# RWKV mixer on one core: inputs of gate and v formed ahead of the decay, joins of the inverse moved up among v's steps, bonus product placed behind the substitution

## The chip, the cores and the metric

The kernel runs as one program on one core of a Trainium2 chip. The metric is device time in microseconds (us), taken over three executions. Five engines run in parallel, each through its own instructions in order: TensorE (PE, matrix products and transposes, with its weight loads PEld), VectorE (DVE), ScalarE (ACT), GpSimd (POOL) and SyncE (SP), which issues the DMAs. They wait for each other by semaphores.

## The reference, cut to what matters

Two layers, each of two SwiGLU feed-forward blocks around a token mixer, and a gated embedding at the end. The second layer's mixer is RWKV-7, with x of 256 positions by 1,024 features, 16 heads of 64, in chunks of 64 positions. Only this mixer is touched:

```
dx = shift(h) - h
r, k, v = (h + dx*mu[n]) @ w_in[n]          # n = 0, 1, 2
xw, xa, xg = (h + dx*mu[n])                 # n = 3, 4, 5
decay = exp(-exp(-softplus(-(w0 + tanh(xw@w1)@w2)) - 0.5))
a = sigmoid(a0 + (xa@a1)@a2);  g = sigmoid(xg@g1) @ g2
kk = heads(k*k_k) / |heads(k*k_k)|;  k = k*(1 + (a-1)*k_a)
S_t = S_{t-1} diag(decay_t) + (S_{t-1} (-kk_t)) (kk_t a_t)^T + v_t k_t^T;  y_t = S_t r_t
bonus = sum(r*k*r_k) * v
out = ((groupnorm(y) + bonus) * g) @ w_out
```

## The kernel before, in words

Activations stand with features on the 128 partitions, eight blocks of 256 positions each. `xprod(n)` (L813) forms one of the six inputs `h + dx*mu[n]` in eight DVE instructions of 128x256, from hnT and dxT. The mixer forms k first (`K`, two halves b of 128 positions), and `knorm(b, ...)` (L889 to L904) normalises it: DVE multiplies out of PSUM, ACT squares, DVE sums and clamps (gn), POOL takes the power and scales. `ktr(b)` transposes the normalised and the plain k on PE. `low` and `l1` are the low-rank products of decay and a; `squares` and `decay` form the decay on ACT and DVE, with two scans (L987).

`r_step(k)` (L1051) is one eighth of r's product. Between its steps stands `triangle(i)`, the chunks' triangular matrices for half of the heads, copied out of PSUM by ACT (L1045, L1046). The inverse of each 64x64 unit triangle starts with a forward substitution on DVE over blocks of 16 (L1090 to L1093) and two transposes (L1094, L1095). Four `join(i)` then join blocks of 16 to 32 and to 64: tiny products on PE, issued in four pieces.

`v_step(k, between)` (L1300) is one eighth of v's product, four matrix products, each followed by one piece of `between`. `inside(k)` (L1274) forms the products within a chunk for one pair of heads (sc), masks them on DVE (L1287) and forms rb. `gate1`, `gate_t` and `gate2` form g; `gains` multiplies g with the norm's gains and the bonus sums of `bo_sums`, which reads k times r (L1269). `tb` transposes b and k and copies them into bn. `stack_v(c)` (L1386) subtracts the mean over 64 from chunk c's v and writes it into the stacked state sv; the means stand in vm (L1383, L1384). `chunk(c)` is the recurrence, four times: PE products, ACT and DVE copies into sv (L1443, L1444), and the state's update on DVE (L1458).

What orders the work: the kernel is written in one order, and a scheduler sets each engine's order from it, by dependences, priorities that follow the text, and estimated costs. `behind(name)` holds what it encloses back until the named instruction has been issued; L collects these names. Large tiles share 20 slots, handed out from a queue of free ones (`slot`, `drop`): a new tile waits until all users of the slot's former tile are done. PSUM's eight banks go round in the same way. `P` and `need` fetch weights: the DMA on SP, a copy on ACT (L154) and a subtraction on DVE (L156) that split each weight in two.

Of the kernel before, what the change touches and what calls it, by code (L numbers as in the profile page):

```python
# [15 lines left out]
D = 1024  # L16
T = 256
NB = 2
# [42 lines left out]
class Trunk:  # L61
# [730 lines left out]
    def rwkv(self, at):  # L792
# [20 lines left out]
        def xprod(n, lo=0, hi=T, ks=range(KT)):  # L813

            if n not in X["x"]:
                X["x"][n] = self.slot("xr")
            hv, dv = g8(X["hnT"]), g8(X["dxT"])
            for k in ks:
                V.scalar_tensor_tensor(xent(n, k)[:, lo:hi], dv[:, k, lo:hi], mu(n, k), hv[:, k, lo:hi], op0=ALU.mult, op1=ALU.add)
# [127 lines left out]
        lt = l1()  # L947
        self.drop(X["x"][3], X["x"][4])
        xprod(0)
        wu_ = self.slot("wu")  # L950
        zt = wu_[:, :1024]
        G.memset(zt, 0.0)
# [139 lines left out]
                            Wd[:, :, 0:t, 0:t].rearrange("p a s i -> p a i s"), op=ALU.mult)  # L1092
            V.tensor_reduce(Wd[:, :, t, 0:t], pr_, axis=AX.X, op=ALU.add)  # L1093
        V.transpose(wv.rearrange("p n s -> p s n"), Wu.rearrange("p t s -> p s t"))  # L1094
        V.transpose(xt.rearrange("p n t -> p t n"), Wu)  # L1095

        def pieces(n, do, last):

# [3 lines left out]
        def join(i):  # L1102

            if i == 0:
                ps = self.bank("q1")

                def do(ns):
                    for n in ns:
                        for o in range(0, 128, 32):
                            mm(ps[o:o + 32, n * 16:(n + 1) * 16], lhsT=nx[o:o + 16, n, :], rhs=wv[o:o + 16, n, 0:16], start=True, stop=True)  # L1110

                def last():
                    S.copy(qn[:, :, 0:16], ps.rearrange("p (n t) -> p n t", t=16))
                    self.unbank(ps)
            elif i == 1:
                ps = self.bank("x1")

                def do(ns):
                    for n in ns:
                        for o in range(0, 128, 32):  # L1120
                            mm(ps[o:o + 32, n * 16:(n + 1) * 16], lhsT=qn[o:o + 32, n, :], rhs=xt[o:o + 32, n, 16:32], start=True, stop=True)

                def last():
                    V.tensor_tensor(xt[:, :, 16:32], ps.rearrange("p (n t) -> p n t", t=16), xt[:, :, 16:32], op=ALU.add)
                    self.unbank(ps)
                    V.transpose(wu_[:, 1024:], md)
                    for o in range(0, 128, 32):
                        c0 = o // 32 % 2 * 32
                        (V.tensor_copy if c0 else S.copy)(xv[o:o + 32, :, c0:c0 + 32], xt[o:o + 32])
            elif i == 2:  # L1130
                ps = [self.bank("q2") for _ in range(2)]

                def do(ns):
                    for n in ns:
                        for o in (0, 64):
                            mm(ps[n // 16][o + 32:o + 64, n % 16 * 32:n % 16 * 32 + 32], lhsT=mo[o:o + 32, n * 32:(n + 1) * 32],
                               rhs=wv[o:o + 32, n, :], start=True, stop=True)

                def last():
                    for hh in range(2):  # L1140
                        for o in (0, 64):
                            (S.copy if o else V.tensor_copy)(qv[o + 32:o + 64, hh * 16:hh * 16 + 16, :], ps[hh][o + 32:o + 64].rearrange("p (n t) -> p n t", t=32))
                    self.unbank(*ps)
            else:
                ps = [self.bank("x2") for _ in range(2)]

                def do(ns):
                    for n in ns:
                        for o in (0, 64):
                            mm(ps[n // 16][o:o + 32, n % 16 * 32:n % 16 * 32 + 32], lhsT=qv[o + 32:o + 64, n, :], rhs=xt[o + 32:o + 64, n, :], start=True, stop=True)  # L1150

                def last():
                    for hh in range(2):
                        for o in (0, 64):
                            (S.copy if o else V.tensor_copy)(xv[o:o + 32, hh * 16:hh * 16 + 16, 32:64], ps[hh][o:o + 32].rearrange("p (n t) -> p n t", t=32))
                    self.unbank(*ps)
            return pieces(32, do, last)
# [90 lines left out]
        rT = self.slot("rT")  # L1248
        for g in range(4):
            S.copy(rT[:, g * 512:(g + 1) * 512], psr[g])  # L1250
        xprod(5)
        gate1()
        xprod(2)
        self.drop(hnT, dxT)
        for m in range(KT):
            S.activation(g8(av)[:, m], g8(av)[:, m], AF.Identity, scale=vec(3)[:, m:m + 1], bias=w0h[:, 8 + m:9 + m])
        V.tensor_tensor(kT, kT, av, op=ALU.mult)
# [7 lines left out]
        for g in range(4):  # L1265
            for h in range(2):
                S.copy(skv[g][half[h], :, h, :, 0:64], gs(ta, g)[half[h]])
                V.tensor_tensor(skv[g][half[h], :, h, :, 64:128], gs(rT, g)[half[h]], gs(gam, g)[half[h]], op=ALU.mult)
        V.tensor_tensor(kT, kT, rT, op=ALU.mult)  # L1269
        self.drop(gam, ta, rT)  # L1270
        rb_ = self.slot("rb")
        rbv = c4(rb_)

        def inside(k):  # L1274

            g, m = k // 2, k % 2
            if m == 0:
                X["rb"] = self.bank("rb")
            psb = X["rb"].rearrange("p (m c t) -> p m c t", m=2, c=4)
            ps = [self.bank("sc") for _ in range(2)]  # L1280
            pv = [t.rearrange("p (c t) -> p c t", c=4) for t in ps]
            for c in range(NCH):
                for h in range(2):
                    mm(pv[h][half[1 - h], c], lhsT=c4(kt)[half[h], k, c], rhs=skv[g][half[h], m, h, c, :], start=True, stop=True)  # L1284
            for h in range(2):
                ho = half[1 - h]
                V.tensor_tensor(skv[g][ho, m, h], pv[h][ho], mk[ho].unsqueeze(1).to_broadcast([64, 4, 128]), op=ALU.mult)  # L1287
            self.unbank(*ps)
            for c in range(NCH):
                for h in range(2):  # L1290
                    hh = half[h]
                    mm(psb[hh, m, c], lhsT=c4(bt)[hh, k, c], rhs=skv[g][hh, m, h, c, 64:128], start=True, stop=True)
            if m:
                V.tensor_tensor(c3(rb_[:, g * 512:(g + 1) * 512]), c3(X["rb"]), mk[:, 64:128].unsqueeze(1).to_broadcast([128, 8, 64]), op=ALU.mult)
                self.unbank(X["rb"])
# [4 lines left out]
        def v_step(k, between=()):  # L1300

            x = xent(2, k)
            w = self.need(at["v"] + k // 2)[0][:, k % 2]
            between = list(between)
            for b in range(NB):
                for q in range(2):
                    mm(psv[b][q], lhsT=x[:, b * 128:(b + 1) * 128], rhs=w[:, q * 512:(q + 1) * 512], start=k == 0, stop=k == KT - 1)  # L1307
                    if between:
                        between.pop(0)()
            if k % 2:  # L1310
                self.release(at["v"] + k // 2)
                if k < 5:
                    P(1, 1)
# [8 lines left out]
        v_step(2)  # L1322
        for n in gate2(1):
            n()
        v_step(3)
        v_step(4)
        xx = self.slot("xx")
        xv = xx.rearrange("p (n t) -> p n t", t=64)
        for o in (32, 96):
            G.memset(xv[o:o + 32, :, 0:32], 0.0)  # L1330
        v_step(5, join(0))
        inside(0)
        inside(1)
        v_step(6, join(1))
        self.drop(nq)
        bo_sums()
        gains()
        inside(2)
        inside(3)
        v_step(7, join(2))  # L1340
        self.drop(X["x"][2])
        vn = self.slot("vn")
        for b in range(NB):
            for q in range(2):
                S.copy(vn[:, b * D + q * 512:b * D + (q + 1) * 512], psv[b][q])
        self.unbank(*psv[0], *psv[1])
        inside(4)
        inside(5)

        bn = [self.slot("bn") for _ in range(2)]  # L1350
        bnv = [t.rearrange("p (c h m t) -> p c h m t", c=2, h=2, t=64) for t in bn]
# [21 lines left out]
        turn.pop(0)()  # L1373
        turn.pop(0)()
        self.drop(bt, kt)

        sv = [self.slot("sv") for _ in range(2)]
        svv = [t.rearrange("p (c m h t) -> p c m h t", c=2, m=8, h=2) for t in sv]
        vv = vn.rearrange("p (b m h t) -> p b m h t", b=2, m=8, h=2)
        vm = self.small(32, "vm", 1)  # L1380
        vmv = vm.rearrange("p (b m h) -> p b m h", b=2, h=2)
        for b in range(NB):
            V.tensor_reduce(vm[:, b * 16:(b + 1) * 16], vn[:, b * D:(b + 1) * D].rearrange("p (h t) -> p h t", t=64), axis=AX.X, op=ALU.add)  # L1383
            V.tensor_scalar(vm[:, b * 16:(b + 1) * 16], vm[:, b * 16:(b + 1) * 16], ck[:, 0:1], 1.0 / 64, op0=ALU.mult, op1=ALU.mult)  # L1384

        def stack_v(c):  # L1386
            rs = half[c % 2]
            for h in range(2):
                V.scalar_tensor_tensor(svv[c // 2][half[1 - h], c % 2, :, h, :], vv[rs, c // 2, :, h, :], ck[rs, 0:1],
                                       vmv[rs, c // 2, :, h].unsqueeze(2).to_broadcast([64, 8, 64]), op0=ALU.mult, op1=ALU.subtract)  # L1390

        for c in range(NCH):
            stack_v(c)
        G.memset(svv[0][EV, 0, :, 0, :], 0.0)
        G.memset(svv[0][OD, 0, :, 1, :], 0.0)

        yo = self.slot("yo")
        yv = yo.rearrange("p (b m h t) -> p b m h t", b=2, m=8, h=2)
# [136 lines left out]
            return ps  # L1535
        chunk(0)
        with behind("c"):
            P(1, 0)
            vgain(0)
        chunk(1)  # L1540
        with behind("c"):
            P(1, 0)
            vgain(1)
        self.drop(X["gn"], X["lg"])
# [135 lines left out]
```

## Time and profile before

| | |
|---|---|
| median of three executions | 1177.98 us (1177.35 to 1180.4) |
| profiled execution | 1183.38 us, span 1181.6 us |
| PE busy | 1151.2 us, 97% |
| DVE busy | 859.1 us, 73% |
| ACT busy | 659.7 us, 56% |
| POOL busy | 72.5 us, 6% |
| weight split on DVE (L156) | 348 times, mean 1223 ns |

Busy is the time in which an engine has an instruction running. The mixer lies in the span from about 745 to 960 us. Over the whole span PE is nearly always busy; in the mixer, stretches follow each other in which a different engine is full, so it has to be read by stretches. The granted clock (PEclk) is 1.00 at 2.4 GHz and 0.50 at 1.2 GHz.

### The profile page before, as it was taken

How to read it: one execution, taken by the hardware profiler on the slowest of the kernel's cores; microseconds unless marked ns; L12 is line 12 of the kernel's file. 1: busy time of each engine (PE TensorE's matmuls, PEld its weight loads, DVE VectorE, ACT ScalarE, POOL GpSimd, SP SyncE). 2: the span in 40 equal slices, each digit the busy share in tenths (PEclk: the TensorE clock that was granted, in tenths of full speed). 3: DMA queues.
4: the chain of work that ended last, by engine and by line, in shares of the span. 5: the costliest groups of instructions: out<-in, count | busy, mean ns of one | idle time of the engine just before them, and what ended most of it. 6: DMA issues, size and time to landing. Idle time of an engine off the chain costs nothing. (4 is left out here: it accounts for less than half of the span.)

```text
span 1181.6 us, 18709 instructions
## 1 busy us (share of the span) xinstructions
PE 1151.2 (97%) x7284; PEld 954.3 (81%) x7284; DVE 859.1 (73%) x1299; ACT 659.7 (56%) x1145; POOL 72.5 (6%) x92
## 2 busy tenths in 40 slices
PE   8999999999999999999999999999998899999997
PEld 6788888888888888888888888777467778888886
DVE  5886666877678666667876666878859898676663
ACT  6665556545476555558755554374226396555553
POOL 0000000010010000001100000230000220000011
PEclk8999999999999999999999999999989999999999
DMA  7886654746586666646766664550300377666510
GB/s 244 292 295 196 190 172 152 253 156 205 186 271 202 194 192 184 192 134 196 248 189 194 193 192 144 178 183 1 125 4 21 108 249 263 193 189 193 177 47 36
DMA packets 58841, 207.78 MB, mean 176 GB/s; under 512 B 6784, under 2 KB 7296, under 8 KB 58496
## 3 DMA queue, kind: packets, MB, share of 16 engines
q1 hardware_dynamic: 58752, 206.59, 54.8%
q8 instruction: 57, 0.93, 0.3%
q14 instruction: 32, 0.26, 0.1%
HBM read 205.51 MB, written 1.05 MB: 175 GB/s over the span
## 5 line engine op out<-in xcount | busy, mean ns | idle before, releaser
L156 DVE TENSOR_TENSOR w<-raw,w 128x1024 fp32r<-128x1024 f32 x348 | 423.6, 1223 | 145.6 <-ACT w L154 139.8
L154 ACT CAST w<-raw 128x1024 fp32r<-128x1024 f32 x348 | 366.3, 1055 | 153.9 <-PE mm L400 68.7
L400 PE MATMUL mm<-xT,w 128*128 128x512 f32 (+1 forms) x2304 | 407.8, 337 | 0.0
L400 PEld LDWEIGHTS mm<-xT,w 128*128 128x128 f32 x2304 | 358.6, 189 | 50.0
L178 PE MATMUL acc<-w,hT 128*128 128x512 f32 x352 | 138.2, 393 | 0.0
L179 PE MATMUL acc<-w,hT 128*128 128x512 f32 x352 | 137.3, 390 | 0.0
L180 PE MATMUL acc<-w,hT 128*128 128x512 f32 x352 | 137.1, 389 | 0.0
L408 ACT COPY pn<-mm 128x256 f32<-128x256 f32 x144 | 46.6, 375 | 93.8 <-PE mm L400 93.8
L409 DVE TENSOR_TENSOR pn<-mm,pn 128x256 f32<-128x256 f32 x144 | 54.4, 418 | 39.3 <-ACT pn L408 39.3
L180 PEld LDWEIGHTS acc<-w,hT 128*128 128x128 f32 x352 | 66.1, 188 | 14.1
L178 PEld LDWEIGHTS acc<-w,hT 128*128 128x128 f32 x352 | 66.2, 188 | 12.6
L179 PEld LDWEIGHTS acc<-w,hT 128*128 128x128 f32 x352 | 66.3, 188 | 12.3
L232 POOL TENSOR_SCALAR rpost<-ss 128x1 f32<-128x1 f32 x15 | 7.5, 500 | 777.9 <-ACT junk L239 777.9
L178 PE MATMUL mm<-w,xT 128*128 128x512 f32 x128 | 51.8, 415 | 2.9 <-ACT w L154 2.6
L289 DVE SCALAR_TENSOR_TENSOR xT<-tr,gT,xT 128x128 fp32r<-128x128 f32 x112 | 35.6, 344 | 24.4 <-ACT xT L288 23.5
L179 PE MATMUL mm<-w,xT 128*128 128x512 f32 x128 | 51.4, 405 | 0.7 <-DVE xT L289 0.5
L412 DVE TENSOR_TENSOR pn<-pn,yc 128x512 f32<-128x512 f32 x72 | 49.7, 691 | 2.0
L180 PE MATMUL mm<-w,xT 128*128 128x512 f32 x128 | 50.9, 403 | 0.0
L179 PE MATMUL z<-w,xT 128*128 128x512 f32 x128 | 49.9, 390 | 0.0
L180 PE MATMUL z<-w,xT 128*128 128x512 f32 x128 | 49.9, 390 | 0.0
L178 PE MATMUL z<-w,xT 128*128 128x512 f32 x128 | 49.7, 393 | 0.0
L288 ACT ACTIVATE xT<-tr,gT 128x128 fp32r<-128x128 f32 x112 | 37.8, 371 | 19.3 <-PE tr L275 14.9
(282 smaller groups left out, 1534.8 us busy)
## 6 DMA issues: line engine op xcount, KB each, us to landing
raw<-in_w SPq DMA_DIRECT2D x264, 512.0 KB, 4.3
raw<-in_win SPq DMA_DIRECT2D x32, 512.0 KB, 4.4
raw<-in_wout SPq DMA_DIRECT2D x16, 512.0 KB, 4.8
raw<-in_wg SPq DMA_DIRECT2D x16, 512.0 KB, 3.9
wf<-in_wrkv SPq DMA_DIRECT2D x8, 1024.0 KB, 5.1
gbc<-in_norm_g SPq DMA_DIRECT2D x9, 512.0 KB, 5.4
raw<-in_wrkv SPq DMA_DIRECT2D x8, 512.0 KB, 3.5
raw<-in_bwout SPq DMA_DIRECT2D x8, 512.0 KB, 3.6
```

Source lines behind the costliest of these rows:

```text
L154: self.high = self.nc.scalar.copy(hh, r[:p, :n])
L156: eng.tensor_tensor(ll, r[:p, :n], hh.bitcast(F32), op=ALU.subtract)
L178: mm(out, lhsT=lh, rhs=rh, start=start, stop=False)
L179: mm(out, lhsT=ll, rhs=rh, start=False, stop=False)
L180: mm(out, lhsT=lh, rhs=rl, start=False, stop=stop)
L232: nc.gpsimd.tensor_scalar(r, a, b, eps, op0=ALU.add, op1=ALU.add)
L288: done = (nc.scalar.activation(hi, v, AF.Copy, scale=gc), nc.vector.scalar_tensor_tensor(lo, v, gc, hi.bitcast(F32), op0=ALU.mult, op1=ALU ...
L289: nc.vector.scalar_tensor_tensor(lo, v, gc, hi.bitcast(F32), op0=ALU.mult, op1=ALU.subtract))
L400: nc.tensor.matmul(ps[i][:, :T] if s else ps[i], lhsT=w[:, sl], rhs=x, start=u + q + s == 0, stop=s + u == 2 and q == 3)
L408: nc.scalar.copy(zi, ps[i][:, T:])
L409: nc.vector.tensor_tensor(zi, ps[i][:, :T], zi, op=ALU.add)
L412: nc.vector.tensor_tensor(z2, z2, rbc.unsqueeze(1).to_broadcast([128, 2, T]), op=ALU.mult)
```

## The change

Five things are moved; no arithmetic is added or removed.

- `xprod(5)` and `xprod(2)`, the inputs of gate and v, stand behind `xprod(0)`, and hnT and dxT are dropped there.
- The joins 0, 1, 2 are carried by v's steps 3, 4, 5 instead of 5, 6, 7; `inside(4)` and `inside(5)` by steps 6 and 7.
- k times r stands behind the last transpose of the substitution (`behind("sub")`).
- The mean of the first half of v and the first two `stack_v` stand ahead of `tb`; the second mean and `stack_v(2)` behind chunk 0, `stack_v(3)` behind chunk 1.
- The slots are handed out in another order as a result, and with them the order of some weight loads.

```diff
@@ behind l1()
         xprod(0)
+        xprod(5)
+        xprod(2)
+        self.drop(hnT, dxT)
@@ the substitution
-        V.transpose(xt.rearrange("p n t -> p t n"), Wu)
+        L["sub"] = V.transpose(xt.rearrange("p n t -> p t n"), Wu)
@@ behind r
-        xprod(5)
         gate1()
-        xprod(2)
-        self.drop(hnT, dxT)
...
-        V.tensor_tensor(kT, kT, rT, op=ALU.mult)
-        self.drop(gam, ta, rT)
+        self.drop(gam, ta)
@@ v's steps
-        v_step(3)
-        v_step(4)
...
-        v_step(5, join(0))
+        v_step(3, join(0))
+        with behind("sub"):
+            V.tensor_tensor(kT, kT, rT, op=ALU.mult)
+        self.drop(rT)
         inside(0)
         inside(1)
-        v_step(6, join(1))
+        v_step(4, join(1))
...
-        v_step(7, join(2))
+        v_step(5, join(2))
+        v_step(6, [lambda: None, lambda: inside(4)])
+        v_step(7, [lambda: None, lambda: inside(5)])
...
-        inside(4)
-        inside(5)
+        mean_v(0)
+        stack_v(0)
+        G.memset(svv[0][EV, 0, :, 0, :], 0.0)
+        G.memset(svv[0][OD, 0, :, 1, :], 0.0)
+        stack_v(1)
@@ ahead of the chunks
-        for c in range(NCH):
-            stack_v(c)
...
         chunk(0)
         with behind("c"):
+            mean_v(1)
+            stack_v(2)
             P(1, 0)
             vgain(0)
         chunk(1)
         with behind("c"):
+            stack_v(3)
             P(1, 0)
             vgain(1)
```

Three places show what the scheduler makes of it. The first is DVE where k's second half is normalised (kn and gn with the highest numbers; xr_6872 is r's input, xr_6881 the gate's and xr_6890 v's). Before:

```order
L901 TENSOR_SCALAR gn_6788<-gn_6788 128x16
L819 SCALAR_TENSOR_TENSOR xr_6872<-dxT_6588,chT,hnT_6587 128x256 x4
L895 TENSOR_TENSOR kn_6906<-k_6779,gbc 128x512
L895 TENSOR_TENSOR kn_6906<-k_6780,gbc 128x512
L898 TENSOR_REDUCE gn_6907<-junk 128x8 x2
L901 TENSOR_SCALAR gn_6907<-gn_6907 128x16
L999 SCALAR_TENSOR_TENSOR eo_6886<-eo_6886,q_537_6885 128x1024
```

Now:

```order
L901 TENSOR_SCALAR gn_6788<-gn_6788 128x16
L819 SCALAR_TENSOR_TENSOR xr_6872<-dxT_6588,chT,hnT_6587 128x256 x4
L819 SCALAR_TENSOR_TENSOR xr_6881<-dxT_6588,chT,hnT_6587 128x256 x8
L819 SCALAR_TENSOR_TENSOR xr_6890<-dxT_6588,chT,hnT_6587 128x256 x8
L895 TENSOR_TENSOR kn_6924<-k_6779,gbc 128x512
L895 TENSOR_TENSOR kn_6924<-k_6780,gbc 128x512
L898 TENSOR_REDUCE gn_6925<-junk 128x8 x2
L901 TENSOR_SCALAR gn_6925<-gn_6925 128x16
L1002 SCALAR_TENSOR_TENSOR eo_6904<-eo_6904,q_539_6903 128x1024
```

All sixteen products stand ahead of kn, gn and the decay, which begins with eo.

The second is PE ahead of r (tr are transposes of k, l the low-rank products, r the first of r's product). Before:

```order
L967 MATMUL l_552_6961<-pn,wf_6808 128x256
L967 MATMUL l_553_6962<-pn,wf_6808 128x256
L913 MATMUL tr_6971<-ident,kn_6906 128x128 x4
L913 MATMUL tr_6977<-ident,kn_6906 128x128 x4
L913 MATMUL tr_6983<-ident,kn_6906 128x128 x4
L913 MATMUL tr_6989<-ident,kn_6906 128x128 x4
L1055 MATMUL r_6997<-xr_6872,wf_6816 128x256 x2
```

Now:

```order
L970 MATMUL l_554_6979<-pn,wf_6808 128x256
L913 MATMUL tr_6989<-ident,kn_6924 128x128 x4
L970 MATMUL l_553_6970<-pn,wf_6808 128x256 x2
L970 MATMUL l_555_6980<-pn,wf_6808 128x256 x2
L913 MATMUL tr_6995<-ident,kn_6924 128x128 x4
L913 MATMUL tr_7001<-ident,kn_6924 128x128 x4
L913 MATMUL tr_7007<-ident,kn_6924 128x128 x4
L1058 MATMUL r_7015<-xr_6872,wf_6816 128x256 x2
```

Four low-rank products have moved behind the first transposes of k's second half; r stands behind all of them in both.

The third is DVE between chunk 0's update (sv from st) and chunk 1's copies (sv from us). Before:

```order
L1458 TENSOR_TENSOR sv_8079<-st_8132,gC 64x4x64 x2
L156 TENSOR_TENSOR w_8201<-raw,w_8201 128x1024
L1244 TENSOR_TENSOR vn_7846<-vn_7846,gn_7343 128x512 x2
L1245 TENSOR_TENSOR vn_7846<-vn_7846,lg_7719 128x512 x2
L1492 TENSOR_REDUCE gv<-k_8235 128x4
L1492 TENSOR_REDUCE gv<-k_8238 128x4
L1444 COPY sv_8079<-us_8210 64x4x64
```

Now:

```order
L1460 TENSOR_TENSOR sv_7880<-st_8113,gC 64x4x64 x2
L1357 TENSOR_REDUCE vm<-vn_7875 128x16
L156 TENSOR_TENSOR w_8188<-raw,w_8188 128x1024
L1358 TENSOR_SCALAR vm<-vm,ck 128x16
L1247 TENSOR_TENSOR vn_7875<-vn_7875,gn_7340 128x512
L1363 SCALAR_TENSOR_TENSOR sv_7881<-vn_7875,ck,vm 64x8x64 x2
L1248 TENSOR_TENSOR vn_7875<-vn_7875,lg_7698 128x512
L1247 TENSOR_TENSOR vn_7875<-vn_7875,gn_7340 128x512
L1494 TENSOR_REDUCE gv<-k_8228 128x4
L1248 TENSOR_TENSOR vn_7875<-vn_7875,lg_7698 128x512
L1494 TENSOR_REDUCE gv<-k_8231 128x4
L1446 COPY sv_7880<-us_8203 64x4x64
```

The mean of v's second half (vm) and two stack products (sv_7881 from vn) have come in between.

## Rows read from the trace of the kernel before

**Rows 1.** The page's head.

```profile
span 1181.6 us, 18709 instructions
```

**Rows 2.** Stretches: length, busy us by engine (instructions), granted clock, DMA share, GB/s.

```profile
786.00:818.00 32.00, 31.85 (x256) 27.52 (x254) 28.10 (x32) 19.13 (x38) 1.80 (x1) 1.00 0.23 79
818.00:849.00 31.00, 28.78 (x94) 14.57 (x94) 30.58 (x61) 11.11 (x22) 1.89 (x2) 1.00 0.25 85
849.00:882.00 33.00, 30.81 (x811) 18.68 (x810) 16.29 (x20) 5.79 (x10) 0.71 (x2) 0.84 0.11 35
882.00:904.00 22.00, 17.85 (x403) 15.27 (x396) 20.75 (x35) 13.96 (x34) 0.33 (x1) 1.00 0.01 3
904.00:945.00 41.00, 37.43 (x633) 31.94 (x634) 36.67 (x68) 16.84 (x38) 10.76 (x8) 0.96 0.29 92
```

**Rows 3.** Timeline of DVE ahead of the decay: start, us, instruction, [idle before].

```profile
769.97 1.66 DVE L819 SCALAR_TENSOR_TENSOR xr<-dxT,chT,hnT 128x256 f32<-128x256 f32 x4
772.01 1.29 DVE L895 TENSOR_TENSOR kn<-k,gbc 128x512 f32<-128x512 f32 x2 [0.39 <-PE k L180]
...
782.29 1.22 DVE L999 SCALAR_TENSOR_TENSOR eo<-eo,q 128x1024 f32<-128x1024 f32 x1 [6.44 <-ACT eo L994]
```

**Rows 4.** Timeline of ACT, same stretch.

```profile
779.76 1.10 ACT L993 ACTIVATE q<-tw 128x1024 f32<-128x1024 f32 x1
```

**Rows 5.** Timeline of POOL, k's second half.

```profile
775.93 2.90 POOL L902 TENSOR_TENSOR gn<-gn,mhalf 128x16 f32<-128x16 f32 x1 [0.74 <-DVE gn L901]
778.91 1.90 POOL L904 TENSOR_TENSOR kn<-kn,gn 128x1024 f32<-128x1024 f32 x1
```

**Rows 6.** Timeline of PE ahead of r.

```profile
780.19 2.22 PE L967 MATMUL l<-pn,wf 64*128 64x256 f32 x16
782.33 0.66 PE L913 MATMUL tr<-ident,kn 128*128 128x128 f32 x4
783.82 1.63 PE L913 MATMUL tr<-ident,kn 128*128 128x128 f32 x12 [0.83 <-ACT kk L914]
785.54 4.80 PE L1055 MATMUL r<-xr,wf 128*128 128x256 f32 x21
```

**Rows 7.** Timeline of PE: behind r, in the joins, ahead of the chunks.

```profile
820.22 4.58 PE L1171 MATMUL g<-wf,xr 128*128 128x160 f32 x32 [2.37 <-ACT rT L1250]
...
857.99 0.33 PE L1292 MATMUL rb<-sk,bt 64*64 64x64 f32 x4 [1.96 <-issue]
...
885.14 0.66 PE L1357 MATMUL tb<-ident,bt 128*128 128x128 f32 x4
...
898.33 0.42 PE L1415 MATMUL us<-sv,sk 128*64 128x64 f32 x4 [2.70 <-DVE sv L1389]
```

**Rows 8.** Chain that ended last, among v's steps: start, us, what.

```profile
824.80 3.43 PE v L1307 x8
...
849.87 1.06 PE v L1307 x2
...
859.84 2.00 PE v L1307 x2
...
882.16 0.69 PE sc L1284 x5
```

**Rows 9.** Timeline of ACT ahead of chunk 0.

```profile
888.33 4.45 ACT L1361 COPY bn<-tb 64x256 f32<-64x256 f32 x12 [4.83 <-DVE bn L1361]
...
900.47 0.65 ACT L1417 COPY k<-us 128x256 f32<-128x256 f32 x2
901.86 0.79 ACT L1443 COPY sv<-us 64x256 f32<-64x256 f32 x2 [0.75 <-issue]
```

**Rows 10.** Timeline of DVE: mean, stack products, chunk 1's update.

```profile
892.78 1.20 DVE L1383 TENSOR_REDUCE vm<-vn 128x16 f32<-128x1024 f32 x1
...
897.44 6.14 DVE L1389 SCALAR_TENSOR_TENSOR sv<-vn,ck,vm 64x512 f32<-64x512 f32 x8
...
912.16 1.78 DVE L1458 TENSOR_TENSOR sv<-st,gC 64x256 f32<-64x256 f32 x4 [0.37 <-PE st L1453]
```

More of the change, by code (lines that the diff above doesn't have):

```diff
@@ L1346, in rwkv, with mean_v, stack_v @@
         self.unbank(*psv[0], *psv[1])
-        inside(4)
-        inside(5)
+        sv = [self.slot("sv") for _ in range(2)]
+        svv = [t.rearrange("p (c m h t) -> p c m h t", c=2, m=8, h=2) for t in sv]
+        vv = vn.rearrange("p (b m h t) -> p b m h t", b=2, m=8, h=2)
+        vm = self.small(32, "vm", 1)
+        vmv = vm.rearrange("p (b m h) -> p b m h", b=2, h=2)
+        def mean_v(b):
+            V.tensor_reduce(vm[:, b * 16:(b + 1) * 16], vn[:, b * D:(b + 1) * D].rearrange("p (h t) -> p h t", t=64), axis=AX.X, op=ALU.add)
+            V.tensor_scalar(vm[:, b * 16:(b + 1) * 16], vm[:, b * 16:(b + 1) * 16], ck[:, 0:1], 1.0 / 64, op0=ALU.mult, op1=ALU.mult)
+        def stack_v(c):
+            rs = half[c % 2]
+            for h in range(2):
+                V.scalar_tensor_tensor(svv[c // 2][half[1 - h], c % 2, :, h, :], vv[rs, c // 2, :, h, :], ck[rs, 0:1],
+                                       vmv[rs, c // 2, :, h].unsqueeze(2).to_broadcast([64, 8, 64]), op0=ALU.mult, op1=ALU.subtract)
+        mean_v(0)
[3 more added lines that the diff above has]
+        stack_v(1)
         bn = [self.slot("bn") for _ in range(2)]
@@ L1375, in rwkv @@
         self.drop(bt, kt)
[L1377 to L1390, printed above, removed]
-        for c in range(NCH):
-            stack_v(c)
-        G.memset(svv[0][EV, 0, :, 0, :], 0.0)
-        G.memset(svv[0][OD, 0, :, 1, :], 0.0)
         yo = self.slot("yo")
```

## The prediction

> **What bounds the kernel now.** I read the busy time by stretch first, and in it the recurrent mixer alone, since no instruction outside it moves. The reader is to see that the bound changes hands [rows 2]: TensorE (PE) is busy 31.85 of 32 us while r is formed, 28.78 of 31 us under the substitution, and 30.81 of 33 us in the joins. Then VectorE (DVE) is full: 20.75 of 22 us and 36.67 of 41 us in the chunks. An edit therefore counts only on PE up to the joins and only on DVE behind them. The second thing to see is the granted clock: 0.84 in the joins' 33 us, so 33 x 0.16 x 2 = 10.6 us of them ran at 1.2 instead of 2.4 GHz. The timelines of each engine and the chain of waits then give the sizes. Small waits of off-path engines, on SP or POOL, I left alone.
>
> **The change, part by part.** All times are of the profiled execution: span 1181.6 us [rows 1], 1183.38 us with the 1.78 us around it, 5.4 us above the median of 1177.98 us. I work out a difference on the profiled execution and add it to the median.
>
> *1. Products of gate and v ahead of the decay.* One product lasts 1.66 / 4 = 0.415 us, so sixteen are 6.6 us [rows 3]. The order puts them behind r's last four and ahead of the normalisation of k's second half. DVE does have an idle stretch here, 6.44 us in front of the decay, and I first took it for the cover. But it lies behind that normalisation, not in front. So the first kn product starts at 771.63 + 6.6 = 778.3 instead of 772.01, 6.3 us later. Between its two squares ScalarE (ACT) now has tanh and the 1.10 us square of the decay [rows 4]: 1.0 us more. So GpSimd (POOL) starts on the sum gn 7.3 us later than at 775.93, at 783.2; its two instructions (2.90 and 1.90 us) end 4.9 us behind that [rows 5], at 788.1. Behind it stand PE's sixteen transposes of that half (twelve take 1.63 us, so 2.2 us) and now four low-rank products (half of 2.22 us, 1.1 us) [rows 6]. r starts at 791.4 or a little later, instead of 785.54: **+6.0 us**. The decay on DVE starts some 1 us later and keeps pace with PE, since PE reaches both triangles 6 us later too. From r on PE has no gap, so the 6.0 us count in full; 1.5 us by which the normalisation was early (done at 780.81, first used at 782.33) are already in them. Bounds: 4.8 us (6.3 less that 1.5) and 7.3 us.
>
> *2. The clock behind that wait.* PE now stands some 6 us: what it has ahead of that half is done by 782.33 today and hardly later then, and the half comes at 788.1. The trace has no such wait inside the mixer. After 1.96 us the clock fell; after 2.37 us and after 2.70 us it stayed at 2.4 GHz [rows 7, 2]. So the length alone decides nothing here, but 6 us is far beyond all three. The one stretch at half speed in the joins lasted 10.6 us; half of that, 5.3 us, is the upper bound, nothing the lower. Since part of the stretch passes in the wait and r's dense products follow, I take half the bound: **+2.5 us**.
>
> *3. The wait for the gate's inputs goes.* PE waited 2.37 us ahead of g [rows 7] though r's banks were free; the first product of x5 stood on DVE behind the transpose of the triangle. That input is now ready, and g starts on r's heels: **-2.4 us**. The substitution on DVE also sheds sixteen products, k times r and one weight split, so it ends further ahead of the joins than now; it is no bound.
>
> *4. Joins two steps earlier.* v's fourth step now carries the first join instead of the sixth. Two steps of 3.43 us [rows 8] move behind the third join: **-6.9 us** up to there (part 6 gives most back).
>
> *5. Waits within the joins.* PE waited 1.96 us between inside(0) and inside(1) for a bank that DVE empties [rows 7]. The order now has a v product there, and other work lasts until the bank is free: **-2.0 us**. lg's slot is now freed only by v's fourth step, so DVE's masks come a little later; I take less than that v product. Without that wait I expect no fall of the clock. A pair of v's instructions takes 2.00 us at half speed and 1.06 us at full [rows 8]; three and a half pairs lose 3.3 us, half of the 10.6 us would be 5.3 us, and I take **-4.2 us**. The Trainium skill (TensorE: Matmul & The Clock Gate, Part 1: The HAM clock gate) says the clock follows how busy the array has lately been. By that rule parts 2 and 5 go as I have them; by the rows alone, where a wait of 1.96 us lowered it and one of 2.70 us did not, part 5 stays open, and it is the first rival.
>
> Up to the end of the third join (882.16 us now) that is 6.0 + 2.5 - 2.4 - 6.9 - 2.0 - 4.2 = -7.0 us.
>
> *6. From the third join to the first chunk.* Two v steps (6.9 us) and inside(4) and inside(5) (882.16 to 885.14, 3.0 us [rows 7, 8]) now come here, 9.9 us, and ACT's copies of b and k follow about 0.9 us later, 10.8 us behind the join. Now they start 6.2 us behind it, at 888.33, since DVE was late [rows 9]: +4.6 us. From there to ACT's copy at 900.47 is 12.1 us of the same work in both. Then DVE's copy into sv started 3.1 us behind, since eight stack products (6.14 us) held DVE until 903.58 [rows 10]; ACT's half of that copy went at 901.86, 1.4 us behind, and so will DVE's: -1.7 us. Four of the eight and a mean now run while PE does v's last steps, where DVE waits for inside(4) and inside(5). **+2.9 us.**
>
> *7. Into the chunks.* The other mean (1.20 us its sum, 1.4 us with its scaling) and four stack products (6.14 / 8 x 4 = 3.1 us) go behind the chunk's chain. Between chunks 0 and 1 DVE waits only 0.37 us ahead of its update, and over the 41 us it is idle for little more than 4 [rows 2, 10]. So 1.4 + 1.5 = **+2.9 us** and then **+1.5 us**. The first split of the output weights also moves in, 1.2 us; behind chunk 3 DVE waits on POOL for longer than that, so the eighth split costs nothing there. Cover gone, it is +1.2 us.
>
> The moved k times r sits on DVE behind the substitution, ahead of gx, where DVE afterwards waits for PE: 0. Uncovered it costs some 2.4 us, twice the 1.20 us of a pass over half as many elements. On SP the fourth load of v now waits for the gate's weights; it is issued over 20 us before v's seventh step: 0.
>
> Sum: -7.0 + 2.9 + 2.9 + 1.5 = **+0.3 us, 1178.3 us**. That is no change: about 0.3%, 3.5 us, is what a measurement of this kernel can tell from none.
>
> **The rivals.** *The clock falls in the joins all the same* (slower). The joins' small products stay as they are, and the 1.96 us wait did no more than other waits that left the clock alone; against it, the wait goes. It decides from the second join on, costs the 4.2 us of part 5: 1182.5 us. *DVE isn't the bound in the chunks* (faster): each chunk has a chain over PE and ACT, and if that ends last the stack products fit under it, -4.4 us: 1173.9 us. For it speaks the 0.37 us wait; against it, 36.67 of 41 us busy. *r does not run slow* after its wait (part 2 is 0): 1175.8 us, within the bound. *The late start is not paid at all*: part 1 would have to be covered by DVE, but PE is busy 31.85 of 32 us there; parts 1 and 2 gone, 1169.8 us.
>
> **How the numbers follow.** Forecast 0.42, r at full speed 0.08, the clock in the joins 0.32, the hidden chunks 0.12, the start unpaid 0.06. Of the first, 0.03 may end over the bound through part 1's upper end and the eighth split (+2.5 us on top, and r's 5.3 us). Faster 0.12 + 0.06 = 0.18; slower 0.32 + 0.03 = 0.35; same 0.47. The range takes in the slower rival with r's upper bound (1182.5 + 2.8 = 1185.3) and the hidden chunks with a lower bound of part 1 (1173.9 - 1.2 = 1172.7), and leaves out the unpaid start: 1172.5 to 1185.5 us. The likeliest case's own range is 1175 to 1182.
>
> **What the profile after would show.** Part 1: DVE goes from xr to kn without a wait, POOL's pow starts near 783 and r near 791.5; r at 786 would refute it. Part 2: a granted clock under 1 around 790. Part 3: g right behind r. Part 5: clock 1 through the joins, no wait over 1 us between the blocks. Part 6: ACT's long row of bn copies some 11 us behind the third join. Part 7: DVE without idle from chunk 0's copy to chunk 3. I am wrong above all if the normalisation of k's second half does not hold PE, or if DVE has slack in the chunks.

## The result, and the profile after

| | before | after |
|---|---|---|
| median | 1177.97 us (1177.35 to 1180.4) | 1198.16 us (1197.46 to 1199.53) |
| ratio | | 1.0165 [1.0151, 1.0179] |
| profiled execution | 1183.38 us, span 1181.6 us | 1197.76 us, span 1195.9 us |
| mean granted clock, profiled execution | 0.989 | 0.981 |

20.2 us slower, where no change was forecast: far above the range. The mixer starts at another time in each execution, by some 4 us, so I read all times from the start of its low-rank row on PE (L926). Three rows of before, PE ahead of r:

```profile
771.91 3.67 PE L926 MATMUL l<-xr,wf 128*64 128x256 f32 x30
775.50 0.66 PE L913 MATMUL tr<-ident,kn 128*128 128x128 f32 x4
776.09 2.33 PE L967 MATMUL l<-pn,wf 64*128 64x256 f32 x16
```

r began there at 785.54 [rows 6], 13.63 us later. After, on PE:

```profile
768.98 3.67 PE L926 MATMUL l<-xr,wf 128*64 128x256 f32 x30
776.86 1.11 PE L913 MATMUL tr<-ident,kn 128*128 128x128 f32 x4 [4.21 <-POOL kn L904]
777.90 3.76 PE L970 MATMUL l<-pn,wf 64*128 64x256 f32 x16
...
791.30 1.12 PE L913 MATMUL tr<-ident,kn 128*128 128x128 f32 x4 [5.90 <-POOL kn L904]
...
798.63 3.62 PE L1058 MATMUL r<-xr,wf 128*128 128x256 f32 x16
```

29.65 us: r is 16.0 us late. PE waits twice for POOL's scaling of k, once per half, and behind the first wait the sixteen low-rank products take 3.76 us instead of 2.33. POOL, in the same stretch:

```profile
767.21 3.08 POOL L902 TENSOR_TENSOR gn<-gn,mhalf 128x16 f32<-128x16 f32 x1 [1.22 <-DVE gn L901]
770.37 6.44 POOL L904 TENSOR_TENSOR kn<-kn,gn 128x1024 f32<-128x1024 f32 x1
785.79 2.91 POOL L902 TENSOR_TENSOR gn<-gn,mhalf 128x16 f32<-128x16 f32 x1 [8.98 <-DVE gn L901]
788.77 2.47 POOL L904 TENSOR_TENSOR kn<-kn,gn 128x1024 f32<-128x1024 f32 x1
```

L904 took 1.90 us before [rows 5]; now the first takes 6.44 and the second 2.47. What stands beside them, on DVE (first the products, then kn's second half, its sums, and the decay):

```profile
767.05 7.99 DVE L819 SCALAR_TENSOR_TENSOR xr<-dxT,chT,hnT 128x256 f32<-128x256 f32 x20
774.97 1.27 DVE L895 TENSOR_TENSOR kn<-k,gbc 128x512 f32<-128x512 f32 x2
782.13 0.69 DVE L898 TENSOR_REDUCE gn<-junk 128x8 f32<-128x512 f32 x1 [5.89 <-ACT junk L897]
...
789.52 2.80 DVE L1005 SCALAR_TENSOR_TENSOR eo<-eo 128x1024 f32<-128x1024 f32 x1
```

The scaling ends at 776.81, 1.77 us behind the last product (767.05 + 7.99 = 775.04): about its own length. And ACT, on which DVE's sum waits 5.89 us:

```profile
778.01 0.59 ACT L914 COPY kk<-tr 128x512 f32<-128x512 f32 x1 [4.56 <-PE tr L913]
780.01 0.84 ACT L973 ACTIVATE tw<-l,w0h 128x256 f32<-128x256 f32 x2 [1.42 <-PE l L970]
780.74 0.84 ACT L980 ACTIVATE a<-l,chT 128x256 f32<-128x256 f32 x2
781.46 0.64 ACT L897 ACTIVATE junk<-kn 128x512 f32<-128x512 f32 x1
...
784.12 0.67 ACT L897 ACTIVATE junk<-kn 128x512 f32<-128x512 f32 x1
```

The same two squares before:

```profile
772.80 0.63 ACT L897 ACTIVATE junk<-kn 128x512 f32<-128x512 f32 x1 [3.94 <-DVE kn L895]
...
774.28 0.64 ACT L897 ACTIVATE junk<-kn 128x512 f32<-128x512 f32 x1
```

The first square of k's second half could go once the first of the two kn is there, 0.7 us behind 774.97, but stands behind a copy of PE's first transposes and behind tanh and sigmoid of the low-rank products. So the first half's blocked scaling holds PE, PE holds ACT, ACT holds the second half.

Later stages, after (read as [rows 2], with a window ahead of them; the granted clock is the last number but two), then the chunks' updates on DVE, which answer to [rows 10]:

```profile
760.00:786.00 26.00, 21.18 (x110) 15.21 (x109) 17.94 (x47) 9.48 (x19) 10.68 (x4) 0.87 0.28 90
786.00:818.00 32.00, 26.70 (x168) 22.78 (x169) 30.83 (x33) 19.94 (x39) 6.97 (x3) 0.84 0.36 132
849.00:882.00 33.00, 30.83 (x754) 18.83 (x753) 22.61 (x23) 4.30 (x7) 1.05 (x2) 0.90 0.19 67
904.00:945.00 41.00, 34.05 (x692) 29.62 (x690) 33.12 (x61) 23.48 (x55) 5.25 (x6) 0.88 0.15 49
```

```profile
914.98 0.88 DVE L1460 TENSOR_TENSOR sv<-st,gC 64x256 f32<-64x256 f32 x2 [0.58 <-PE st L1455]
...
924.20 1.78 DVE L1460 TENSOR_TENSOR sv<-st,gC 64x256 f32<-64x256 f32 x4 [0.43 <-PE st L1455]
...
935.67 1.78 DVE L1460 TENSOR_TENSOR sv<-st,gC 64x256 f32<-64x256 f32 x4
```

From L926's start, in us, with a second profile of before (the ninth experiment) and the two parts run alone:

| | before | before, again | after | joins alone | stack alone |
|---|---|---|---|---|---|
| r starts | 13.63 | 13.63 | 29.65 | 13.64 | 13.64 |
| third join copied | 110.98 | 108.29 | 116.10 | 102.88 | 108.15 |
| chunk 0 updated | 134.67 | 132.72 | 146.88 | 131.26 | 131.55 |
| chunk 1 | 142.03 | 140.07 | 157.00 | 140.09 | 142.12 |
| chunk 2 | 151.95 | 149.99 | 168.47 | 150.00 | 153.58 |
| last row of the output yo (L1504) | 170.26 | 168.30 | 187.59 | 169.11 | 171.88 |

Against the second profile the mixer is 187.59 - 168.30 = 19.3 us longer, nearly all of the 20.2.

### The profile page after: what moved, and what is told of

It is laid out like the page before. It is cut to its first block, busy times and chain, and to the rows that moved or that the text cites. A ratio compares the mean times of both kernels' runs of the same rounds, so it can differ in the third digit from the quotient of the medians.

```text
span 1195.9 us, 18700 instructions
## 1 busy us (share of the span) xinstructions
PE 1158.7 (97%) x7284; PEld 960.8 (80%) x7284; DVE 862.2 (72%) x1299; ACT 659.6 (55%) x1145; POOL 77.9 (7%) x92
## 4 chain that ended last, share of the span: by engine, by line
PE 84%; DVE 7%; POOL 2%; ACT 2%; issue 2%; DMA 2%; SPq 0%; POOLq 0%; DVEq 0%; ACTq 0%
PE mm L400 34%; PE acc L178 7%; PE acc L179 7%; PE acc L180 7%; PE z L178 2%; PE z L179 2%; PE z L180 2%; PE v L1306 2%; PE r L1058 2%; PE mm L179 2%; DMA raw<-in_w 2%; PE mm L180 2%; DVE w L156 2%; PE mm L178 2%; PE tr L275 1%
## 5 line engine op out<-in xcount | busy, mean ns | idle before, releaser
L178 PEld LDWEIGHTS acc<-w,hT 128*128 128x128 f32 x352 | 66.2, 188 | 12.6
L416 ACT CAST hT<-k 128x256 fp32r<-128x256 f32 x72 | 28.9, 402 | 34.7 <-DVE k L414 34.6
```

The costliest lines, as they stand in the source:

```text
L178: mm(out, lhsT=lh, rhs=rh, start=start, stop=False)
L416: nc.scalar.copy(hi, sg)
```

## The experiments

**1. Products back** (1185.57 us, 1181.69 to 1188.85; ratio 1.0057 [1.0038, 1.0076]). The changed kernel with:

```diff
         xprod(0)
-        xprod(5)
-        xprod(2)
-        self.drop(hnT, dxT)
...
+        xprod(5)
         gate1()
+        xprod(2)
+        self.drop(hnT, dxT)
```

> The changed kernel with the products of gate and v back behind r, as before; all else stays changed. Theory A (GpSimd's first scaling of k is kept waiting by VectorE's run of products, and with it PE's transposes, ACT and the second half): the scaling L904 takes 1.9 us again instead of 6.44, PE has no wait over 1 us ahead of r, the 16.0 us by which r was late go and the 2.4 us wait ahead of g returns: 1198.2 - 16.0 + 2.4 = 1184.6 us, 1182 to 1187. Theory B (only the order of VectorE's queue counts, as in the prediction, 6.0 + 2.5 - 2.4 us): 1192 us. Theory C (the loss arises behind the third join): 1192 us or more, with r early.

r starts 13.63 us behind L926, as before, and both scalings take 1.90 us. 12.6 us come back. The rest of the change still costs 7 us, which the prediction's parts 4 to 7 did not have.

**2. Products alone** (1191.75 us; 1.0109 [1.0086, 1.0132]): before, with the edit of the first experiment the other way round.

> The kernel before with the products of gate and v alone moved ahead of the decay; joins, bonus product and stack products stay where they were. Theory A: the first scaling L904 takes 6 us or more, PE waits twice for some 4 and 6 us ahead of r at a granted clock under 1, r is some 16 us late and g follows without its wait: 1178.0 + 16.0 - 2.4 = 1191.6 us, 1188 to 1194. Theory B: 1178.0 + 6.1 = 1184 us. Theory C: within 3 us of 1184 with a late start, the rest of the loss missing.

+13.2 us. First scaling 6.44 us, PE waits 4.21 and 5.64 us, r at 29.68: the same picture in a kernel in which nothing else moved. Theory A's size, not the 6.1 us of my parts 1 to 3.

**3. Products with one input** (1201.0 us; 1.0189 [1.0174, 1.0204]).

```diff
-                V.scalar_tensor_tensor(xent(n, k)..., dv[...], mu(n, k), hv[...], ...)
+                for _ in range(2):   # n = 2 and 5 only
+                    V.tensor_scalar(xent(n, k)..., dv[...], mu(n, k), 1.0, ...)
```

> The changed kernel, but each of the sixteen products of gate and v is replaced by two VectorE instructions that read one tensor instead of two (the addition of h is left out of these two inputs). The order of every queue and the dependences stay. Theory A (two tensor inputs on VectorE keep GpSimd from SBUF): the first scaling L904 takes 1.9 to 2.5 us instead of 6.44 and ends before VectorE's run of products does; PE's first wait goes; the second half stays late by the queue: r some 8 us late instead of 16, about 1190 us. Theory B (order of the queue alone, or GpSimd slow for a reason of its own): L904 still above 6 us or its length without effect, 1196 to 1199 us.

Missed, in an instructive way. DVE and POOL:

```profile
770.25 8.49 DVE L821 TENSOR_SCALAR xr<-dxT,chT 128x256 f32<-128x256 f32 x32
```

```profile
768.84 9.95 POOL L906 TENSOR_TENSOR gn<-gn,mhalf 128x16 f32<-128x16 f32 x1 [1.22 <-DVE gn L905]
778.87 1.90 POOL L908 TENSOR_TENSOR kn<-kn,gn 128x1024 f32<-128x1024 f32 x1
```

Beside this form even the power, 3.08 us beside the two-input products, takes 9.95 and ends 0.05 us behind the run. So the block does not need two inputs; theory A as I had put it falls, and the next control has to be another.

**4. Products in DVE's gap** (1183.12 us; 1.0038 [1.0024, 1.0052]).

```diff
         knorm(1, p1)
+        xprod(5)
+        xprod(2)
+        self.drop(hnT, dxT)
```

> The changed kernel with the products of gate and v written behind the normalisation of k's second half, so that most of them run in VectorE's idle time ahead of the decay. Theory A: the first scaling takes 1.9 us, the second does not start moving before VectorE's products end, and ends some 1.9 us behind the last; r is 1 to 4 us later than in the first experiment, g follows without a wait: 1183 to 1187 us. Theory B: both scalings 1.9 us, r on time and g without its wait: 1184.6 - 2.4 = 1182 us or, if only the queue order cost anything, 1190 us.

In time at theory A's lower end, and the second scaling does what it says: it starts at 778.95 beside the last products, which end at 780.07, and takes 2.88 us: 1.76 behind them. But r is on time (13.64), as theory B had it, and g follows it without a wait.

**5. Products reading PSUM** (1192.27 us; 1.0107 [1.0083, 1.013]).

```diff
-                V.scalar_tensor_tensor(..., dv[...], mu(n, k), hv[...], ...)
+                hk = X["pk"][:, lo:hi] if n in (2, 5) else hv[:, k, lo:hi]
+                V.scalar_tensor_tensor(..., dv[...], mu(n, k), hk, ...)
```

> The changed kernel, but the sixteen products of gate and v read PSUM (a bank of k) in place of h, so that each has one input in SBUF and one in PSUM (the addition of h is left out of these two inputs). Order and count of the instructions stay. The third experiment replaced them by twice as many instructions with one input in SBUF, and GpSimd was held even longer (its power took 9.95 us and ended with the run). Theory A (VectorE's instructions on SBUF of both kinds keep GpSimd out): beside these, the power takes 3 us and the first scaling L904 1.9 to 2.2 us again, ending some 5 us before VectorE's run; PE waits no more than 2 us there; the second half stays late by the queue, r some 8 us late: 1188 to 1193 us. Rival (any unbroken run of VectorE holds GpSimd): L904 6 us or more, 1196 to 1200 us.

DVE and POOL:

```profile
770.24 6.35 DVE L820 SCALAR_TENSOR_TENSOR xr<-dxT,chT,k 128x256 f32<-128x256 f32 x16
```

```profile
768.82 3.08 POOL L903 TENSOR_TENSOR gn<-gn,mhalf 128x16 f32<-128x16 f32 x1 [1.21 <-DVE gn L902]
771.98 1.90 POOL L905 TENSOR_TENSOR kn<-kn,gn 128x1024 f32<-128x1024 f32 x1
```

The same instruction and count on DVE, at nearly the same length (16 in 6.35 us, against 20 in 7.99); only where one input lies has changed, and the scaling takes 1.90 us in the middle of the run. This settles the block. r is 22.45 - 13.63 = 8.8 us late, so 7.2 of the 16.0 us went with the block. The 8.8 us lie near the 6.0 + 2.5 of the prediction, but not by its terms. The power of the second half's sum on POOL:

```profile
785.40 3.86 POOL L903 TENSOR_TENSOR gn<-gn,mhalf 128x16 f32<-128x16 f32 x1 [11.52 <-DVE gn L902]
```

That is 14.80 us behind L926, 10.8 us later than before where the prediction had 7.3, and the granted clock is 0.50 from 784 to 796 us. The orders of ACT and PE came out otherwise here, with eight of the sixteen transposes ahead of the wait for POOL. That the sums agree is partly luck.

The Trainium skill (SBUF — State Buffer, Who interferes with whom) states such a lock between VectorE and GpSimd, for VectorE instructions with two SBUF inputs and for some one-input forms. The scaling agrees for the first (6.44 us against 1.90) and the power for the second (9.95 us against 3.08). That the power took only 3.08 us beside two-input products, against 2.90 alone [rows 5], is not explained by it. I had read that rule and left it out, since the one scaling in [rows 5] stood beside nothing that showed it.

**6. Joins alone** (1179.88 us; 1.0006 [0.9991, 1.002]): before, with the diff's edits to v's steps, inside and the bonus product, and no other.

> The kernel before with the joins two steps earlier, inside(4) and inside(5) in v's last steps and the bonus product behind the substitution; products and stack as before. Theory D (the profile of before held a stretch at half speed in the joins that most timed runs of it do not have, so the 4.2 us for it were never there to be gained, and new waits lower the clock elsewhere): 1179 to 1183 us at a mean granted clock of 0.989 to 0.993 (before: 0.994). Rival (the gains of the prediction are there and the stack loses them): -6.9 - 2.0 - 4.2 + 4.6 + 2.9 = -5.6 us, 1173 us, clock 0.995 or more.

No change: theory D. PE's wait among the joins' products is still there, and behind it the clock still falls:

```profile
846.63 0.37 PE L1110 MATMUL q<-wu,nq 16*32 16x16 f32 x23 [1.34 <-issue]
```

```profile
848.00:852.00 4.00, 4.00 (x114) 3.96 (x116) 3.51 (x4) 0.59 (x1) 0.00 (x0) 0.54 0.53 171
852.00:856.00 4.00, 4.00 (x49) 2.21 (x47) 1.71 (x4) 0.00 (x0) 0.00 (x0) 0.61 0.27 97
```

**7. Stack alone** (1184.27 us; 1.0048 [1.003, 1.0065]): before, with the diff's edits to mean_v and stack_v only.

> The kernel before with the mean and the stack products alone moved: one mean and four products ahead of the transposes of b and k, the others behind chunk 0 and chunk 1. The prediction's terms: -1.7 (stack out of the way of the first chunk) + 2.9 + 1.5 = +2.7 us, 1181 us. Theory D (the clock falls in chunk 0 behind the new wait for ACT's bn copies): 1182 to 1186 us at a clock of 0.988 to 0.991. Rival (the stack costs nothing, the loss is in the joins): 1177 to 1179.5 us at 0.994.

+4.8 us: in theory D's range, but not by its mechanism. By the table, against the second profile of before: 1.2 us won up to chunk 0, then (142.12 - 131.55) - 7.35 = 3.2 us and 11.46 - 9.92 = 1.5 us lost. The granted clock was 1.00 in 882 to 904 us, and what is lost is lost between the chunks, where DVE has its mean and its products to do, as in part 7. Some 0.5 of the 3.2 us is another thing: DVE waits 0.87 us for PE ahead of chunk 1's update instead of 0.37, and the granted clock was 0.72 in 908 to 912 us.

**8. Gap alone** (1175.83 us; 0.9972 [0.9957, 0.9986]): before, with the edit of the fourth experiment in place of the products' old place.

> The kernel before with the products of gate and v alone moved, behind the normalisation of k's second half. From the fourth experiment: the first scaling 2.2 us, the second 2.9 us instead of 1.9, r about 1 us later, g without its wait of 2.4 us: 1178.5 - 2.4 + 1 = 1177 us, 1175.5 to 1178.5. Rival (PE's wait ahead of g only moves to the joins, or the clock falls): 1179 us or more.

Faster than both kernels: g's wait goes, r stays on time.

**9. Before, again** (one execution, 1180.69 us): the kernel before, unaltered.

> The kernel before, profiled once more. Theory D (the profile behind the prediction was an execution 5.4 us above the median, and a part of that, not of the kernel, was in its stretch at half speed and in a late start of the mixer): this one has a span nearer 1177 us, a mean granted clock of 0.992 to 0.995, a half-speed stretch in the joins that is there but shorter than 10.6 us, and again a wait of 1 to 2 us without a releaser among the joins' small products. Rival (the profile was typical and the stretch belongs to the kernel in full): span near 1181 us and about 10 us at half speed.

Half a hit: the span of 1178.9 us is above what I expected, but the stretch has moved; the wait among the joins' small products is there (1.36 us). g, behind a wait as in [rows 7], and the windows of this second profile:

```profile
819.39 6.26 PE L1171 MATMUL g<-wf,xr 128*128 128x160 f32 x32 [2.36 <-ACT rT L1250]
```

```profile
818.00:849.00 31.00, 29.61 (x92) 16.07 (x93) 30.58 (x61) 10.39 (x20) 1.89 (x2) 0.94 0.26 85
849.00:882.00 33.00, 30.93 (x880) 20.56 (x879) 18.32 (x24) 6.63 (x11) 1.05 (x2) 1.00 0.11 36
```

Here the clock fell behind the 2.36 us wait and hardly in the joins (the 0.84 of [rows 2] is now 1.00). It also fell ahead of chunk 0 (0.92 in 882 to 904 us, where [rows 2] has 1.00) and not in the chunks (1.00 in 904 to 945, there 0.96). The same program falls at other places in other executions. Of the 65 executions of before that were timed beside the experiments, 64 had mean clocks of 0.990 to 0.996 and one had 0.989, as had the one that the prediction rests on.

**10. Gap and joins** (1176.25 us; 0.9983 [0.9971, 0.9994]): the edits of the sixth and eighth together.

> The products in VectorE's gap and the joins two steps earlier, stack as before. If the parts add up (gap -3.6, joins +0.4 us): 1175 to 1176.5 us, no gain over the gap alone. If the joins' earlier place pays once g follows r at once: 1170 to 1173 us. If the clock falls behind g or in chunk 0 as in the fourth experiment: 1178 us or more.

The parts add up; the joins bring nothing here either.

**11. Gap, first join spread** (1175.04 us; 0.9967 [0.9955, 0.9979]).

```diff
-        v_step(4)
+        j0 = join(0)          # in eight pieces
+        v_step(4, j0[:4])
...
-        v_step(5, join(0))
+        v_step(5, j0[4:])
```

> The products in VectorE's gap as in the eighth experiment, and the first join spread over two of v's steps, in eight pieces of sixteen products instead of four of thirty-two, so that half as many small products stand between two of v's; nothing else moves. Theory E (the wait without a releaser and the fall of the clock come from the dense run of small products): the 1.2 to 2 us wait goes and the half-speed stretch shrinks: 1175.8 - 1.2 - up to 3.5 = 1171 to 1174.6 us. Rival (both come from inside(0) and inside(1), or from elsewhere): the wait and the stretch stay, 1175 to 1176.5 us.

In its profile the wait is gone and the clock is 1.00 through the joins (in the eighth's profile it was at 0.50 in 852 to 856 us):

```profile
848.00:852.00 4.00, 4.00 (x106) 1.89 (x106) 0.00 (x0) 0.12 (x1) 0.00 (x0) 1.00 0.30 99
852.00:856.00 4.00, 3.94 (x94) 2.87 (x94) 3.05 (x5) 0.46 (x1) 0.00 (x0) 1.00 0.02 6
```

Its third join comes 103.47 us behind L926, the eighth's 106.41: theory E's place and size, from one profile of each. The time is the rival's: the median lies 0.8 us under the eighth's, but each is 3.6 us under the kernel before that was measured beside it, and the intervals overlap. The two are not told apart. It is the lowest median of all.

**12. PE's wait filled** (1183.09 us; 1.0034 [1.0022, 1.0047]).

```diff
-            for k in range(KT):
+            for k in [*range(KT)] * 2:      # in l1
```

> The changed kernel with the first low-rank product l1 formed twice over (the second time from the start, so that the values stay), 3.7 us of dense work on PE inside its 4.2 us wait for the first scaling. If the fallen clock is a part of the late start: the sixteen l products behind the wait take 2.2 us instead of 3.76, ACT and the second half come 1 to 3 us earlier, r is 13 to 15 us late instead of 16.0, 1195 to 1197 us. If only the waits count: r 16 us late, 1198 us; if the second pass is paid: 1200 us or more.

All three expectations missed, on the good side: 15 us back, by adding work. The blocked scaling is still 6.44 us long:

```profile
778.60 0.66 PE L913 MATMUL tr<-ident,kn 128*128 128x128 f32 x4 [0.78 <-POOL kn L904]
779.19 2.00 PE L970 MATMUL l<-pn,wf 64*128 64x256 f32 x16
...
789.12 14.08 PE L1058 MATMUL r<-xr,wf 128*128 128x256 f32 x64
```

The clock stays at 1 up to r and behind it, and r is 18.42 - 13.63 = 4.8 us late. But the scheduler, which takes l1 for longer now, also put ACT's squares ahead of its copies. One more run parts the two.

**13. ACT's order alone** (1190.3 us; 1.0094 [1.0078, 1.011]). The changed kernel, with knorm(1, p1) written ahead of low and this around ktr's copies, tanh and sigmoid:

```diff
+                L["sq"] = S.activation(j, ..., AF.Square)
...
+                    with behind("sq"):
                         S.copy(dst[...], ps...)
```

> The changed kernel with ScalarE's order alone altered ahead of r: the two squares of k's second half and its copies stand ahead of the copies of PE's transposes and of the low-rank tanh and sigmoid, as they came to stand in the twelfth experiment; no second pass of l1, so PE's wait of 4.2 us for the first scaling stays. Theory F (in the twelfth experiment it was ScalarE's order that gave the 15 us back: the held transposes no longer hold the second half's squares): r 5 to 9 us late, 1184 to 1190 us. Theory G (it was the clock: PE falls to half speed behind its wait and everything behind it with it): r 13 us late or more, 1195 us or more.

ACT and PE:

```profile
776.56 0.63 ACT L897 ACTIVATE junk<-kn 128x512 f32<-128x512 f32 x1 [2.27 <-DVE kn L895]
```

```profile
777.68 0.76 PE L913 MATMUL tr<-ident,kn 128*128 128x128 f32 x4 [4.20 <-POOL kn L904]
778.37 3.53 PE L971 MATMUL l<-pn,wf 64*128 64x256 f32 x16
...
791.80 13.98 PE L1061 MATMUL r<-xr,wf 128*128 128x256 f32 x64
```

r is 21.98 - 13.63 = 8.35 us late, and POOL starts on the second half's sum 10.00 us behind L926 instead of 16.81, though the first half's scaling is as late as ever. In this run and the twelfth PE's order changed too: all low-rank products stand ahead of the second half's transposes again. So of the 16.0 us the order, on ACT and with it on PE, makes 7.7 (16.0 - 8.35), and the filled wait with its clock 3.6 (8.35 - 4.8). The 4.8 left are the lower bound of part 1, but that the queue on DVE alone makes them is not shown: in the twelfth run the second half's scaling ends at 785.80, and PE comes to its transposes at 785.92, behind work of its own that is late as well. Both theories hold a share; the other half of the 7.2 us between this run and the twelfth arises behind r, where the granted clock in 849 to 882 us was 0.90 here and 1.00 there.

## Why the prediction was wrong, point by point

**Part 1, the late start: the step that failed.** "Between its two squares ScalarE (ACT) now has tanh and the 1.10 us square of the decay [rows 4]: 1.0 us more. So GpSimd (POOL) starts on the sum gn 7.3 us later than at 775.93, at 783.2". It starts 16.81 us behind L926 instead of 4.02: 12.8 us later. The queue on DVE makes 5.9 us of this (kn starts 5.99 us behind L926 instead of 0.10; 6.3 were forecast), and the work between the two squares 1.2 (2.66 us from one to the other instead of 1.48; 1.0 was forecast). The other 5.7 us are the first square's, which goes 6.49 us behind kn's start instead of 0.79; this wait the sum had at nothing. I followed the second half along DVE and took the first half's transposes, low-rank products and copies for done by 782.33, as they are in [rows 6]. They were not: the products that delay the second half on DVE also block POOL's scaling of the first half (shown by the fifth experiment), PE stands 4.21 us, and ACT's in-order queue carries that over to the second half (shown by the thirteenth, where the first square goes 0.77 us behind kn). I priced what is queued behind the moved instructions on their own engine, and asked of no other engine what it does in that time.

**Part 2, the clock behind the wait.** Right that it falls, wrong by the number of waits, which is two, and too small in size: behind the second wait PE takes 7.33 us to r (791.30 to 798.63), where part 1 counts 3.3 us of work and part 2 adds 2.5. In sum parts 1 and 2 were 8.5 us; the 8.8 us without the block come about otherwise (fifth experiment).

**Part 3.** g follows r at once after, as forecast; the eighth experiment pays it out.

**Parts 4 and 5, up to the third join: failed too.** From r to the third join the prediction took 2.4 + 6.9 + 2.0 + 4.2 = 15.5 us off; the table gives 97.35 to 86.45, 10.9 us, and only 8.2 against the second profile of before. "PE waited 1.96 us between inside(0) and inside(1) for a bank that DVE empties" was a misreading: the row says "issue", nothing that the profile shows, and the wait goes with the first join's small products wherever these go (among them, 1.93 us after and 1.34 in the sixth experiment; in the profile behind the prediction just behind them). And the 4.2 us were a trait of one execution: I worked out differences on a profile 5.4 us above the median and added them to the median. The first rival, the clock that falls in the joins all the same, was right as a mechanism (0.90 in 849 to 882 us after).

**Part 6: 2.9 us forecast,** 30.78 - 23.69 = 7.1 us in the profiles (6.4 against the second). The joins alone make 4.0 of it, near the 4.6; the 1.7 us that the stack was to give came to 1.0 alone (24.43 - 23.40), and to 0.3 against the first profile (23.69 - 23.40). Of the three, only the second profile had lost clock there (0.92 in 882 to 904 us). In the whole change its four products stand ahead of DVE's copies into bn, for which ACT then waits:

```profile
898.92 3.31 ACT L1383 COPY bn<-tb 64x256 f32<-64x256 f32 x9 [2.28 <-DVE bn L1383]
```

PE then waits 2.14 us for ACT, and chunk 0 runs partly at half speed (0.88 in the window). How much of the remaining 3.4 us (6.4 - 4.0 + 1.0) is that clock was not tried.

**Part 7: right.** +2.9 and +1.5 us forecast; the table has 10.12 - 7.36 = 2.8 and 11.47 - 9.92 = 1.5. DVE is the bound there: all seven profiles of kernels with the whole change behind r (this one and experiments 1, 3, 4, 5, 12 and 13) have 10.12 to 10.14 and 11.46 to 11.48, at granted clocks of 0.83 to 0.92 in 904 to 945 us.

Sum of the three parts run alone: 13.2 + 0.4 + 4.8 = 18.4 of 20.2 us (the rest lies within the intervals), where the prediction had 6.1, 4.6 - 6.9 - 6.2 = -8.5, and 2.7.

## What to carry to other kernels

When a run of instructions is moved on one engine, list what every other engine does during that run, and look for those that share a path to memory with it and for queues that stand behind them, not only for the moved run's own successors. A stretch at half speed in one profile belongs to that execution: compare its time with the median first, and take a second profile before a gain is booked from it. A wait that the trace puts down to nothing is not to be given a cause by its neighbourhood.

## What the runs showed of the hardware

- GpSimd's scaling of 128x1024 took 1.90 us beside VectorE products with one input in PSUM, and 6.44 within a run of twenty that read SBUF twice, ending 1.77 us behind the last. It got nearly nowhere between two of them. GpSimd's power of 128x16 took 9.95 us beside thirty-two one-input instructions on SBUF, but 3.08 beside two-input products and 2.90 alone; why the two differ is open. VectorE can lose as well: its instruction beside the second scaling took 2.80 us instead of 1.23.
- Adding 3.5 us of dense products (7.12 - 3.67 of L926) to a wait of PE made the kernel 15 us faster than without; another order on ACT, and with it on PE, gave 7.9 of the 15.1 by itself (experiments 12 and 13).
- Sixty-four small products between two of v's (0.73 us) go with a wait of 1.1 us or more, in one or two pieces, that has no releaser, in all profiles of this case but one; thirty-two (0.44 us) went without. What PE waits for is open. The Trainium skill (Runtime: NRT & Kernel Launch, Instruction fetch mechanics) says that each engine's instructions come over a DMA queue of its own while it runs; no run here shows that this is the wait.
